# Residues of four kinds of split made by VectorE instead of GpSimd, and one softmax step issued later

## The chip, the cores and the metric

The kernel runs on one core of a Trainium2 chip. The metric is the device time of one execution in microseconds (us). Most executions of one kernel agree within 0.3%; three runs of the kernel before are given below, and one further execution was profiled.

## The reference

One inference step of a decoder layer. 1024 prompt tokens and 8 sample tokens pass through the same weights; the model is 1024 wide and everything is float32.

```python
h = rmsnorm(x, norm_mix_g);  proj = h @ w_in           # -> u, q, k, v, gate, f_low
mixed = concat(pool_mixer(u) , gla(q, k, v, log_f) * silu(gate))
x = x + mixed @ w_out
hm = rmsnorm(x, norm_mem_g); qm = hm @ w_qm            # 4 heads of 256
s = qm . mem_k * 256 ** -0.5; p = softmax(s)           # 256 memory tokens
x = x + (p @ mem_v) @ w_om
hf = rmsnorm(x, norm_ffn_g)
x = x + relu(hf @ w_up) ** 2 @ w_down                  # hidden 4096
```

For the prompt the memory's keys and values come from `mem_prompt`: `mk = mn @ w_km`, `mv = mn @ w_vm`, with `mn` the normed memory. For each of the 8 sample tokens they come from caches, `cache_mem_k` and `cache_mem_v`, of 256 tokens, 4 heads, 256 wide. The gated linear attention (`gla`) is a recurrence over chunks of 64 tokens. Outputs are the two results after a last norm, the memory's keys and values, and the recurrent states.

## The kernel before

**Arithmetic.** Every float32 operand of a large product is held as two parts in the rounded matmul format `F32R`: `hi`, the rounded value, and `lo`, the residue `x - hi`. A product is three matmuls: hi by hi, hi by lo, lo by hi. The two parts are made by `split`: ScalarE (ACT) writes `hi` (line 157), and another engine subtracts (line 158). That engine is VectorE (DVE) unless the caller passes `eng=G`, which is GpSimd (POOL).

**Stages.** After the memory's keys come two stretches that matter here. In the first, some 245 to 438 us into the span, the recurrence runs beside the last projections, the pooling mixer, the memory's values and the product with `w_out`. In the second, 438 to 627 us, cross-attention runs beside the product with `w_qm` and the start of that with `w_om`. The MLP takes the rest.

**What sets the order.** The two stretches are written as strings of steps, `GLA` and `ATTN` (lines 48 to 57). A token with a letter issues a step; a dot issues nine matmuls (six by `hi` weights, three by `lo`, 344 columns each) of the product that was begun last. Each step issues its whole chain, on all engines; a scheduler then fixes one order of instructions for each engine from what the strings recorded, and every engine works through its own list in that order. An instruction whose operand is late stops all behind it on its engine.

**Steps of the strings that are touched.** In `GLA`, `m` is `mv_unit`: 128 KB of `w_vm` for each of its two k-blocks, split 128x512 at once, and 12 matmuls into the PSUM tile `accv` (line 730); there are 16 units. In `ATTN`:

- `kH` is `load_kv`: the keys and values of head H, `kvr`, split into `kv` by two 128x1024 halves taken as one instruction.
- `VHb` is `sample_v4`: cached values of four sample tokens, DMA into `vt`, then four splits 128x512 into `vs`. There are eight, so 32 residues.
- `sHb` is `sample_scores`: VectorE multiplies cached keys `kt` with the broadcast query `qb` and sums, four instructions for each pair of sample tokens (line 856), into `ssc`.
- `wH` is `sample_p`: TensorE turns `ssc` into `ptss` (two transposes, line 862), then a softmax. `zH` is `sample_pt`: transposes of the result into `ptt` (line 895), split into `pz`. `pHn` is `sample_pv`: the sample context `psv` from `vs` and `pz` (line 911).
- `gC` begins a column block of the product with `w_qm`; its end makes `qm`, `q` and a small copy `qsm` (lines 928, 158, 933). `qC` turns `qsm` into `ptq` (line 939) and sends it to DRAM, from where `qb` is read.
- `SHt`, `THt`, `CHt` are the prompt's scores, the transposes `ptpp` with their split `pT`, and the context `accpv` (line 977). `N` is the norm's sum `pts` (line 255), read by VectorE into `v` (line 258).

Other names in the rows: `acc` with `wqmh`, `wqml` are the matmuls of the product with `w_qm` (line 194); `vt` with line 584 is the scaled value projection of the recurrence, `ws` with line 437 a sum over tiles of `w_down`, `kinv` and line 655 the opening of a chunk's scores in PSUM tile `accg`. PSUM tiles of the kinds `acc...` in `accp`, and the small ones in `mp`, have two buffers each, so a product can't begin before an older tile has been read.

Of the kernel before, what the change touches and what calls it, by code (L numbers as in the profile page):

```python
# [50 lines left out]
       "o2 a4 t2 b4 t3 . n4 m ... a5 o3 m b5 .... n5 a6 o4 b6 t4 t5 m . n6 . a7 x . m . b7 o5 ... n7 . o6 .... t6 "  # L51
       "o7 . t7 ...")
ATTN = ("g0 ..... V00 N ... k0 g1 ........ q0 g2 .. q1 .. S00 .... T00 g3 . S01 ..... C00 T01 s00 V04 . s02 . s06 "
# [7 lines left out]
def body(ctx, tc, a, o):  # L61
    nc = tc.nc
    V, A, G, PE, SY = nc.vector, nc.scalar, nc.gpsimd, nc.tensor, nc.sync
# [12 lines left out]
    def slot(shape, dt=F32, name="slot"):  # L76
        return S.tile(shape, dt, tag="s", name=name)
# [4 lines left out]
    def f(x):  # L82
        return x.bitcast(F32)
# [70 lines left out]
    def split(dst_hi, dst_lo, src, scale=None, eng=None):  # L154

        if scale is None:
            A.copy(out=dst_hi, in_=src)  # L157
            (eng or V).tensor_tensor(out=dst_lo, in0=src, in1=f(dst_hi), op=ALU.subtract)  # L158
        else:
            A.activation(out=dst_hi, in_=src, func=AF.Copy, scale=scale)  # L160
            V.scalar_tensor_tensor(out=dst_lo, in0=src, scalar=scale, in1=f(dst_hi), op0=ALU.mult, op1=ALU.subtract)
# [554 lines left out]
    def mv_unit(n):  # L716

        c, k0 = n // 4, 2 * (n % 4)
        if k0 == 0:
            mv_out["acc"] = mp.tile([P, MC, 256], F32, tag="m", name="accv")  # L720
        acc = mv_out["acc"]
        raw = wp.tile([P, 2, 256], F32, tag="raw", name="wvm", bufs=3)
        SY.dma_start(raw, a["w_vm"][0][k0 * P:(k0 + 2) * P, c * 256:(c + 1) * 256].rearrange("(k p) c -> p k c", p=P))
        hi = wp.tile([P, 2, 256], F32R, tag="whi", name="wvmh", bufs=3)
        lo = wp.tile([P, 2, 256], F32R, tag="wlo", name="wvml", bufs=3)
        split(hi, lo, raw, eng=G)
        for kk in range(2):
            for q, (x, y) in enumerate(((0, hi), (0, lo), (1, hi))):
                for m in range(MC):
                    PE.matmul(acc[:, m, :], mn[x][:, k0 + kk, m * P:(m + 1) * P], y[:, kk, :],  # L730
                              start=(k0 == 0 and kk == 0 and q == 0 and m == 0),
                              stop=(k0 == KC - 2 and kk == 1 and q == 2 and m == MC - 1), skip_group_check=True)
        if k0 == KC - 2:
            t = sm.tile([P, MC, 256], F32, tag="k2", name="mvq")
            for m in range(MC):
                A.activation(out=t[:, m, :], in_=acc[:, m, :], func=AF.Copy, scale=mr[:, 1, m:m + 1])
            SY.dma_start(mv_d[:, :, c * 256:(c + 1) * 256], t)
            SY.dma_start(o["mv"][0, 0, :, c, :].rearrange("(m p) d -> p m d", p=P), t)
# [54 lines left out]
    def out_done(acc, c, i):  # L793
# [11 lines left out]
        if c == 0:  # L805
# [3 lines left out]

    units = list(range(16))  # L810
    STEPS = {'a': gla1, 'b': gla2, 'n': gla3, 't': gla4, 'm': lambda: mv_unit(units.pop(0)), 'P': pool_out,
             'o': out_half, 'v': lambda: values_turn(3, t), 's': sample_state, 'x': sample_out}
    wpool = load_w(a["w_pool"][0].rearrange("g p c -> (g p) c"), "wpool")
# [53 lines left out]
    KV = {}  # L867

    def load_kv(h):
        kvr = tmp.tile([P, 2, 2, MT], F32, tag="t", name="kvr")  # L870
        SY.dma_start(kvr[:, 0], mkT_d[:, 2 * h:2 * h + 2, :])
        SY.dma_start(kvr[:, 1], mv_d[:, :, h * MD:(h + 1) * MD])
        KV[h] = slot([P, 2, 2, 2, MT], F32R, "kv")
        split(KV[h][:, 0], KV[h][:, 1], kvr, eng=G)

    SV, SP = {}, {}

    def sample_v4(h, *b4s):
        for b4 in b4s:
            vt = slot([P, 4, MC, MD], F32, "vt")  # L880
            for m in range(MC):
                SY.dma_start(vt[:, :, m, :],
                             a["cache_mem_v"][0, b4:b4 + 4, m * P:(m + 1) * P, h, :].rearrange("b p d -> p b d"))
            for bb in (0, 2):
                vs = SV[h, b4 + bb] = slot([P, 2, 2, MC, MD], F32R, "vs")
                for b in range(2):
                    split(vs[:, 0, b], vs[:, 1, b], vt[:, bb + b], eng=G)

    def sample_pt(h):

# [95 lines left out]
    def sample_ctx(h):  # L986
        for j in range(2):
            hi, lo = C[2 * h + j]
            split(hi[:, TP:], lo[:, TP:], VS[h][:, j, :])

    STEPS = {'g': queries_mem, 'N': lambda: tokens_sum(ss1.ss, "r2"), 'q': sample_q, 'k': load_kv, 'S': scores,
             'T': turn, 'C': context, 's': sample_scores, 'V': sample_v4, 'w': sample_p, 'z': sample_pt, 'p': sample_pv,
             'x': sample_ctx, 'O': lambda c: add_ctx(c)}

# [445 lines left out]
```

## Time and profile before

| | |
|---|---|
| three runs | 1399.91, 1406.67, 1414.76 us (median 1406.67) |
| profiled execution | 1404.68 us; its span 1403.0 us, so 1.7 us lie around the span |
| mean granted clock of TensorE | 0.982 |
| TensorE busy | 1331.8 us, 95% of the span |
| VectorE busy | 913.4 us, 65% |
| ScalarE busy | 580.6 us, 41% |
| GpSimd busy | 218.4 us, 16% |

The profile is one execution. It gives for each engine the instructions with start and duration, the idle time ahead of an instruction and what ended it, and the clock granted to TensorE; 1.00 is 2.4 GHz and 0.50 is 1.2 GHz. Engines overlap, so a busy share alone tells no cost; a wait of an engine that the end depends on does. In the stretches above that engine is TensorE: the matmuls of one product follow another with no pause except where a row shows idle time.

### The profile page before, as it was taken

How to read it: one execution, taken by the hardware profiler on the slowest of the kernel's cores; microseconds unless marked ns; L12 is line 12 of the kernel's file. 1: busy time of each engine (PE TensorE's matmuls, PEld its weight loads, DVE VectorE, ACT ScalarE, POOL GpSimd, SP SyncE). 2: the span in 40 equal slices, each digit the busy share in tenths (PEclk: the TensorE clock that was granted, in tenths of full speed). 3: DMA queues.
4: the chain of work that ended last, by engine and by line, in shares of the span. 5: the costliest groups of instructions: out<-in, count | busy, mean ns of one | idle time of the engine just before them, and what ended most of it. 6: DMA issues, size and time to landing. Idle time of an engine off the chain costs nothing. (4 is left out here: it accounts for less than half of the span.)

```text
span 1403.0 us, 22658 instructions
## 1 busy us (share of the span) xinstructions
PE 1331.8 (95%) x8734; PEld 1237.0 (88%) x8734; DVE 913.4 (65%) x1443; ACT 580.6 (41%) x1065; POOL 218.4 (16%) x229
## 2 busy tenths in 40 slices
PE   6999999899999989999999999998998999999996
PEld 6999999789999978878977799898986899999886
DVE  5776655886555577853768577677776654675663
ACT  6531122444345333533557445444445432342522
POOL 2143100331023022442200011112110000000000
PEclk9999999999999999999999999999998999999998
DMA  8846542674465436555435556555649955986671
GB/s 267 258 121 190 151 151 83 195 223 164 148 203 160 142 117 208 170 198 175 130 118 164 169 180 206 174 189 175 210 167 368 312 187 160 288 252 188 219 211 61
DMA packets 287557, 261.39 MB, mean 186 GB/s; under 512 B 13496, under 2 KB 239682, under 8 KB 287321
## 3 DMA queue, kind: packets, MB, share of 16 engines
q1 hardware_dynamic: 275289, 226.08, 52.0%
q0 software_dynamic: 6400, 21.17, 4.1%
q10 hardware_dynamic: 5760, 12.68, 2.5%
q8 instruction: 69, 1.13, 0.3%
q14 instruction: 39, 0.32, 0.1%
HBM read 195.04 MB, written 64.85 MB: 185 GB/s over the span
## 5 line engine op out<-in xcount | busy, mean ns | idle before, releaser
L1107 PE MATMUL acc<-T,wuph 128*128 128x260 f32 (+1 forms) x1408 | 288.6, 317 | 13.0 <-DVE c L1155 9.2
L1275 PE MATMUL accd<-F,wdnh 128*128 128x260 f32 (+1 forms) x1344 | 266.3, 310 | 6.1 <-ACT wdnh L157 6.1
L1107 PEld LDWEIGHTS acc<-T,wuph 128*128 128x128 f32 x1408 | 214.4, 191 | 33.8 <-ACT c L1158 5.2
L1275 PEld LDWEIGHTS accd<-F,wdnh 128*128 128x128 f32 x1344 | 201.1, 189 | 20.2 <-ACT wdnh L157 6.3
L1107 PE MATMUL acc<-T,wupl 128*128 128x260 f32 (+1 forms) x704 | 180.6, 317 | 3.6 <-DVE wupl L158 3.6
L1275 PE MATMUL accd<-F,wdnl 128*128 128x260 f32 (+1 forms) x672 | 167.4, 311 | 2.8 <-DVE wdnl L158 2.7
L1107 PEld LDWEIGHTS acc<-T,wupl 128*128 128x128 f32 x704 | 116.8, 191 | 13.1 <-DVE wupl L158 4.8
L1275 PEld LDWEIGHTS accd<-F,wdnl 128*128 128x128 f32 x672 | 109.5, 189 | 11.7 <-DVE wdnl L158 4.7
L157 ACT CAST wdnh<-wdn 128x1024 fp32r<-128x1024 f32 x52 | 54.8, 1053 | 129.8 <-PE accd L1275 124.2
L157 ACT CAST F<-fac 128x1040 fp32r<-128x1040 f32 (+2 forms) x61 | 59.9, 986 | 63.0 <-DMA fac<-fd 49.9
L158 DVE TENSOR_TENSOR F<-fac,F 128x1040 fp32r<-128x1040 f32 (+2 forms) x61 | 68.9, 1143 | 18.6 <-ACT F L157 18.0
L194 PE MATMUL acc<-c,womh 128*128 128x260 f32 (+2 forms) x384 | 80.8, 321 | 0.0
L158 DVE TENSOR_TENSOR wdnl<-wdn,wdnh 128x1024 fp32r<-128x1024 f32 x52 | 63.5, 1221 | 23.6 <-ACT wdnh L157 23.6
L194 PE MATMUL acc<-hm,wqmh 128*128 128x344 f32 x384 | 74.6, 328 | 0.0
L157 ACT CAST wuph<-w 128x512 fp32r<-128x512 f32 x64 | 38.6, 617 | 67.5 <-PE acc L1107 65.2
L194 PEld LDWEIGHTS acc<-c,womh 128*128 128x128 f32 x384 | 59.4, 188 | 6.4 <-ACT womh L157 0.8
L194 PEld LDWEIGHTS acc<-hm,wqmh 128*128 128x128 f32 x384 | 63.3, 192 | 0.6
L1111 ACT ACTIVATE c<-c 128x512 f32<-128x512 f32 (+1 forms) x64 | 40.2, 636 | 55.2 <-DVE c L1161 24.9
L158 POOL TENSOR_TENSOR vs<-vt,vs 128x512 fp32r<-128x512 f32 x32 | 47.3, 1506 | 95.2 <-ACT vs L157 91.7
L1259 DVE TENSOR_TENSOR wdn<-wdn 128x1024 f32<-128x1024 f32 x24 | 29.4, 1225 | 41.8 <-DMA wdn<-in_w_down 41.8
L194 PE MATMUL acc<-c,woml 128*128 128x260 f32 (+2 forms) x192 | 49.7, 320 | 0.0
L158 DVE TENSOR_TENSOR wupl<-w,wuph 128x512 fp32r<-128x512 f32 x64 | 42.7, 686 | 4.5 <-ACT wuph L157 4.4
(402 smaller groups left out, 2620.4 us busy)
## 6 DMA issues: line engine op xcount, KB each, us to landing
wdn<-in_w_down SPq DMA_DIRECT2D x64, 512.0 KB
fac<-fd SPq DMA_DIRECT2D x32, 520.0 KB
w<-in_w_up SPq DMA_DIRECT2D x64, 256.0 KB
ws<-in_w_down SPq DMA_DIRECT2D x48, 256.0 KB
fac<-fd SPq DMA_DIRECT2D x19, 512.0 KB
fd<-w POOLq DMA_DIRECT2D x32, 260.0 KB, 2.6
x<-xd SPq DMA_DIRECT2D x16, 516.0 KB
xd<-x SPq DMA_DIRECT2D x16, 516.0 KB
```

What stands on the lines that cost most here:

```text
L157: A.copy(out=dst_hi, in_=src)
L158: (eng or V).tensor_tensor(out=dst_lo, in0=src, in1=f(dst_hi), op=ALU.subtract)
L194: PE.matmul(acc[:, g, :c1 - c0], w, X[k][j][:, c0:c1], start=(k == 0 and i == 0), stop=(k == len(W) - 1 and i == 2))
L1107: PE.matmul(acc, w, t[k // 2][:, k % 2, j, c0:c1], start=(first and k == 0 and i == 0), stop=(k == HK - 1 and i == 2), skip_group_check=True)
L1111: A.activation(out=t, in_=t, func=AF.Relu)
L1259: V.tensor_tensor(out=raw[0], in0=raw[0], in1=raw[1], op=op)
L1275: PE.matmul(acc, W[x][:, k, :], ff[:, y, k % 2, c0:c1], start=(q == 0 and k == 0 and i == 0), stop=(q == 1 and k == UK - 1 and i == 2))
```

## The change

Two edits. `eng=G` is left out of the three calls of `split` in `mv_unit`, `load_kv` and `sample_v4`, so that 16 residues of 128x512, 4 of 128x1024 and 32 of 128x512 are VectorE's. GpSimd keeps its other work. And in `ATTN` the two tokens `w0 z0` move from behind `s04` to behind `g4 .. k1 q2 C01 ..`.

```diff
@@ ATTN @@
 ATTN = ("g0 ..... V00 N ... k0 g1 ........ q0 g2 .. q1 .. S00 .... T00 g3 . S01 ..... C00 T01 s00 V04 . s02 . s06 "
-        "s04 w0 z0 g4 .. k1 q2 C01 .. S10 .... q3 g5 p00 k2 S11 p01 q4 . s12 T10 .. s16 .. C10 s14 . T11 . x0 V10 "
+        "s04 g4 .. k1 q2 C01 .. w0 z0 S10 .... q3 g5 p00 k2 S11 p01 q4 . s12 T10 .. s16 .. C10 s14 . T11 . x0 V10 "
         "s10 . g6 C11 q5 . s20 . w1 s24 .. z1 S20 p10 k3 V14 s26 .... T20 g7 .. S21 .... s22 . T21 . C20 q7 V20 q6 "
@@ def mv_unit(n): @@
-        split(hi, lo, raw, eng=G)
+        split(hi, lo, raw)
@@ def load_kv(h): @@
-        split(KV[h][:, 0], KV[h][:, 1], kvr, eng=G)
+        split(KV[h][:, 0], KV[h][:, 1], kvr)
@@ def sample_v4(h, *b4s): @@
-                    split(vs[:, 0, b], vs[:, 1, b], vt[:, bb + b], eng=G)
+                    split(vs[:, 0, b], vs[:, 1, b], vt[:, bb + b])
```

The scheduler's lists differ in the two stretches alone. Three places matter to what follows.

TensorE, first stretch, where the first unit of the memory's values is multiplied. Before, the first two `accv` matmuls by `hi` weights are followed by this (the 27 `accv` matmuls go on to `kinv`; some rows that only repeat are left out):

```order
L730 MATMUL accv<-wvmh,mn_128 128x256 x2
L730 MATMUL accv<-wvml,mn_128 128x256 x2
L730 MATMUL accv<-wvmh,mn_129 128x256 x2
...
L730 MATMUL accv<-wvmh,mn_129 128x256
L655 MATMUL accg<-ident,kinv 128x128 x2
L521 MATMUL ptp<-ident,ul 23x128
```

and after the change by this:

```order
L730 MATMUL accv<-wvmh,mn_128 128x256 x2
L655 MATMUL accg<-ident,kinv 128x128 x2
L521 MATMUL ptp<-ident,ul 23x128
L659 MATMUL accg<-zb,kinv 128x256 x2
L529 MATMUL accp<-pr,wpoolh 128x344 x3
L529 MATMUL accp<-pr,wpooll 128x344 x3
L730 MATMUL accv<-wvml,mn_128 128x256 x2
L730 MATMUL accv<-wvmh,mn_129 128x256 x2
```

The matmuls with `kinv`, which need the PSUM tile that VectorE's `vt` (line 584) reads last, stand 27 `accv` matmuls earlier, and those are spread over the places behind them.

TensorE, second stretch, around the first head's two transposes `ptss`. Before:

```order
L977 MATMUL accpv<-pT,kv 128x512 x12
L194 MATMUL acc<-hm_3988,wqmh 128x344 x5
L862 MATMUL ptss<-ident,ssc 8x128
L194 MATMUL acc<-hm_3988,wqmh 128x344
L194 MATMUL acc<-hm_3988,wqml 128x344 x3
L194 MATMUL acc<-hm_4041,wqmh 128x344 x6
```

and after:

```order
L939 MATMUL ptq<-ident,qsm 8x128
L977 MATMUL accpv<-pT,kv 128x512 x12
L194 MATMUL acc<-hm_3988,wqmh 128x344 x6
L194 MATMUL acc<-hm_3988,wqml 128x344 x3
L194 MATMUL acc<-hm_4041,wqmh 128x344 x6
L194 MATMUL acc<-hm_4041,wqml 128x344 x3
L194 MATMUL acc<-hm_4094,wqmh 128x344 x6
L194 MATMUL acc<-hm_4094,wqml 128x344 x2
L862 MATMUL ptss<-ident,ssc 8x128
```

Between `accpv` and the first `ptss` stood 5 matmuls of 344 columns, and now stand 26; the transpose `ptq` has moved ahead of `accpv`.

VectorE, start of the second stretch, around the read of the norm's sum. Before:

```order
L281 TENSOR_TENSOR ss<-ss,sq 128x1032
L158 TENSOR_TENSOR wqml<-wqm,wqmh 128x512
L258 TENSOR_SCALAR v<-pts 128x1032
L226 TENSOR_TENSOR vt<-vt,v 128x1032
L158 TENSOR_TENSOR wqml<-wqm,wqmh 128x512
```

and after:

```order
L281 TENSOR_TENSOR ss<-ss,sq 128x1032
L158 TENSOR_TENSOR wqml<-wqm,wqmh 128x512
L158 TENSOR_TENSOR vs<-vt,vs 128x512 x4
L258 TENSOR_SCALAR v<-pts 128x1032
L158 TENSOR_TENSOR wqml<-wqm,wqmh 128x512
L226 TENSOR_TENSOR vt<-vt,v 128x1032
```

The first four residues of cached values stand ahead of `v`. The other seven sets of four stand in the same way between VectorE's older work; the second set is ahead of the first head's last `kt` instructions.

## Rows read from the trace of the kernel before

**Rows 1.** Busy time in windows: length, then busy us of PE, PEld, DVE, ACT, POOL, clock.

```profile
245.00:438.00 193.00, 184.48 (x1213) 174.43 (x1213) 125.33 (x244) 88.09 (x232) 47.47 (x39) 0.98 0.61 191
438.00:627.00 189.00, 176.20 (x1130) 161.55 (x1129) 125.68 (x296) 80.97 (x185) 57.18 (x36) 0.96 0.50 159
...
280.00:315.00 35.00, 32.15 (x210) 28.96 (x211) 28.65 (x79) 16.23 (x58) 11.98 (x13) 0.95 0.72 221
283.00:286.40 3.40, 3.40 (x16) 3.40 (x15) 1.05 (x6) 1.65 (x2) 0.93 (x1) 0.50 0.62 156
498.10:504.80 6.70, 4.91 (x18) 4.75 (x19) 5.27 (x13) 1.27 (x4) 1.10 (x1) 0.50 0.00 0
600.50:607.20 6.70, 5.82 (x28) 3.92 (x29) 3.33 (x7) 4.00 (x12) 1.49 (x2) 0.50 0.47 149
```

**Rows 2.** TensorE's waits, 245 to 438 us: total us, times, longest.

```profile
PE accv L730 <- POOL wvml L158: 2.9, 3, 1.2
PE accp L529 <- DVE rn L228: 2.3, 1, 2.3
```

**Rows 3.** TensorE's waits, 438 to 627 us.

```profile
PE ptss L862 <- DVE kt L856: 6.2, 1, 6.2
PE psv L911 <- DVE pT L158: 2.9, 1, 2.9
PE ptq L939 <- DVE qsm L933: 1.1, 1, 1.1
```

**Rows 4.** Groups by line, whole span: busy us, mean ns, idle before.

```profile
L158 POOL TENSOR_TENSOR vs<-vt,vs 128x512 fp32r<-128x512 f32 x32 | 47.3, 1506 | 95.2 <-ACT vs L157 91.7 <-issue 3.6
L158 DVE TENSOR_TENSOR wupl<-w,wuph 128x512 fp32r<-128x512 f32 x64 | 42.7, 686 | 4.5 <-ACT wuph L157 4.4
...
L158 POOL TENSOR_TENSOR wvml<-wvm,wvmh 128x512 fp32r<-128x512 f32 x16 | 22.7, 1424 | 90.8 <-ACT wvmh L157 74.6 <-issue 9.3 <-DMA wvm<-in_w_vm 5.8
...
L158 DVE TENSOR_TENSOR wd<-wdn,wd 128x1024 fp32r<-128x1024 f32 x4 | 4.9, 1225 | 3.9 <-ACT wd L157 3.9
```

**Rows 5.** The same view, VectorE alone, 438 to 627 us.

```profile
L856 DVE SCALAR_TENSOR_TENSOR kt<-kt,qb 128x256 f32<-128x256 f32 x64 | 37.2, 636 | 8.7 <-DMA kt<-in_cache_mem_k 4.7 <-DMA qb<-qdr 3.9
```

**Rows 6.** Timeline, 489 to 501 us, of TensorE, VectorE, GpSimd and ScalarE.

```profile
499.89 0.38 PE L862 MATMUL ptss<-ident,ssc 128*8 128x128 f32 x1 [6.19 <-DVE kt L856]
...
489.14 0.17 DVE L933 COPY qsm<-qm 128x8 f32<-128x8 f32 x1
491.24 1.52 DVE L856 SCALAR_TENSOR_TENSOR kt<-kt,qb 128x256 f32<-128x256 f32 x1 [1.94 <-DMA kt<-in_cache_mem_k]
...
499.41 0.41 DVE L856 SCALAR_TENSOR_TENSOR kt<-kt,qb 128x256 f32<-128x256 f32 x1
...
491.18 5.54 POOL L158 TENSOR_TENSOR vs<-vt,vs 128x512 fp32r<-128x512 f32 x4 [36.43 <-ACT vs L157]
496.68 2.52 POOL L158 TENSOR_TENSOR kv<-kvr,kv 128x1024 fp32r<-128x1024 f32 x1
...
490.48 2.19 ACT L157 CAST vs<-vt 128x512 fp32r<-128x512 f32 x4 [2.94 <-DMA vt<-in_cache_mem_v]
```

**Rows 7.** Timeline in the first stretch, TensorE and VectorE.

```profile
256.70 0.39 PE L730 MATMUL accv<-wvmh,mn 128*128 128x256 f32 x2
...
258.34 3.45 DVE L437 TENSOR_TENSOR ws<-ws 128x512 f32<-128x512 f32 x2
261.71 1.22 DVE L584 TENSOR_TENSOR vt<-acc,r 128x1032 f32<-128x1032 f32 x1
```

**Rows 8.** Timeline at the start of the second stretch: VectorE, ScalarE, TensorE.

```profile
438.70 1.23 DVE L258 TENSOR_SCALAR v<-pts 128x1032 f32<-128x1032 f32 x1 [2.28 <-PE pts L255]
...
439.00 2.19 ACT L157 CAST vs<-vt 128x512 fp32r<-128x512 f32 x4 [3.30 <-DMA vt<-in_cache_mem_v]
...
442.75 1.11 PE L194 MATMUL acc<-hm,wqmh 128*128 128x344 f32 x6
443.70 0.63 PE L194 MATMUL acc<-hm,wqml 128*128 128x344 f32 x3
```

## The prediction

> **What bounds the kernel now.** I read the table of busy time in windows first. In both stretches that the change touches TensorE is the long engine: 184.48 of 193 us and 176.20 of 189 us, with VectorE at 125 us in each [rows 1]. So time is lost or won in two ways only: TensorE's idle time, 8.5 and 12.8 us, and TensorE at its lower clock. The window table shows three stretches at 0.50 (1.2 GHz), with 3.40, 4.91 and 5.82 us of matmul time in them [rows 1]; at 1.00 (2.4 GHz) the same work takes half, so they cost some 1.7, 2.5 and 2.9 us. The second and the third of them stand right behind waits of 6.19 and 2.9 us.
>
> The table of waits names who ended each idle time. In the first stretch it is GpSimd's `wvml` for 2.9 us in three places, VectorE's `rn` for 2.3 [rows 2]. In the second it is VectorE: `kt` 6.2 us once, `pT` 2.9 once, `qsm` 1.1 once [rows 3]. The timeline around the longest one shows why VectorE was late. Its first `kt` instruction starts at 491.24 and takes 1.52 us, where one at 499.41 takes 0.41. Between the two GpSimd is busy without a break: four residues of cached values from 491.18 for 5.54 us, then `kv` from 496.68 for 2.52 [rows 6]. The group of 64 has a mean of 636 ns [rows 5], so (636 - 420) ns x 64 = 13.8 us of these rows is stretch, and what runs beside the long ones is GpSimd's subtraction. The undisturbed `qsm` copy takes 0.17 us [rows 6]; the wait of 1.1 us on another one is of the same making.
>
> **The change part by part.**
>
> *GpSimd loses 52 residues:* 47.3 + 22.7 us [rows 4] and for `kv` 4 x 2.52 [rows 6], 80 us of its time. It was idle for long in either stretch, so that by itself is worth nothing; what counts is the three waits on `wvml` and the stretched rows.
>
> *VectorE gains them.* The nearest rows are VectorE's own subtractions of the same shapes: 686 ns for 128x512 and 1225 ns for 128x1024 [rows 4]. First stretch: 16 x 0.69 = 11.0 us. Second: 32 x 0.69 + 4 x 1.23 = 27.0 us. Against it stand the stretches that go: in the second at least the 13.8 us; in the first 2.1 us for the two `ws` (3.45 us, for two at 0.69) [rows 7], and I guess 3 in all. VectorE then has about 133 of 193 and 139 of 189 us. On the mean it is far from full, so the place of each residue in its list decides.
>
> The size of what is given back can be weighed against the Trainium skill, "SBUF — State Buffer", section "Who interferes with whom": a VectorE instruction with two SBUF inputs contends with a GpSimd instruction that reads SBUF, and the one issued later is blocked for the other's whole duration. Were each of the 52 residues to block VectorE for its whole length, 80 us would come back instead of the 17 that I count, and VectorE would be lighter than before. The rows show less, since GpSimd often runs beside an idle VectorE. I keep 17.
>
> *The first head's softmax (`w0 z0` with the second set of residues).* Before, TensorE stood from 493.70 to 499.89 at `ptss` [rows 6]. After, VectorE has the four residues ahead of the last seven `kt`. The casts start when the cached values land and end at 492.67 [rows 6]; the last residue ends near 493.5. Then come one `kt` (0.35 from start to start), `q` (1.23, by `v` of the same size) and seven `kt` (2.4): 497.5. TensorE now has 21 more matmuls of 344 columns ahead of `ptss`, 0.16 us each (six from 442.75 to 443.70) [rows 8]: 3.3 us, and `ptq` 0.1, so it arrives at 497.1. It waits some 0.4 to 0.8. Of 6.19 us, 5.4 go, and with them the half clock behind it: +7.9. It keeps a lower end of 0, if `kt` or the landing is as late as now plus the residues.
>
> *`qsm`:* TensorE's wait of 1.1 us [rows 3] goes with the stretch of its copy: +1.1, at least 0. Near 563 us the fifth set of four (2.75 us) comes ahead of `pT` in VectorE's list; its neighbours there shrink too. Between -2.75 and +0.7 I take -0.3.
>
> *`psv`:* the 2.9 us for `pT` [rows 3] and the half clock behind it (2.9) are 5.8 us at most. Ahead of that `pT` stand eight `kt`, which give back some 1.7 us by the mean of the stretch, and up to 4 if they are among the long ones; but in the same stretch VectorE gets two sets of residues, 5.5 us. Between 0 and 5.8 I take +3.0, as most of those residues fall where TensorE has other work.
>
> *Start of the second stretch:* the first four residues stand ahead of `v`. Their casts end at 441.19; the last residue ends near 441.9, `v` at 443.1, where before it ended at 439.93. The product's next tile can start only then, and TensorE wanted it at 442.75 [rows 8]: -0.6, if the cached values land when they did. A later landing goes on one for one.
>
> *First stretch.* The block of 27 `accv` matmuls (0.12 us each by their 256 columns, 3.2 us) no longer covers the wait for `vt`. `vt` ended at 262.93, and some 2.2 us earlier without the stretch of `ws` [rows 7], so 260.7. TensorE arrives at 256.95, behind two matmuls from 256.70 on [rows 7], and waits 3.7 us; it is 2.3 us ahead at `kinv` but owes 3.2 us of work, -0.9. A wait of 2.9 was followed by a half clock above; I count one here, -1.7. On the other side 1.8 us of the `wvml` waits that lie further on go, the owed work can fill most of the wait on `rn` (+1.5), and the half clock at 283 us can go (+1.7). VectorE, 28.65 of 35 us busy from 280 to 315 [rows 1], gets some four residues there, 2.7 us less what GpSimd gave: -1.9. Sum +0.5, between -4.5 and +5.
>
> **Sum:** 7.9 + 1.1 - 0.3 + 3.0 - 0.6 + 0.5 = 11.6 us. The profiled execution took 1404.68 us (span 1403.0), which would become 1393.1; it lies 2.0 us below the median of the three runs, 1406.67, so against that I forecast **1395**. About 1%, 14 us either way, is what measurement can tell from no change.
>
> **Rivals.**
>
> *VectorE becomes the bound where it is densest.* Only `ptss` and `qsm` pay (7.9 + 1.1); `psv` gives nothing, the fifth set costs 1.0, the first stretch 2.8 (block and clock), the start 0.6: gain 4.6, time 1402. For it: 82% busy from 280 to 315 us, and eight sets of 2.75 us standing whole in an in-order list. Against: some 50 us of idle time on VectorE in the second stretch. The Trainium skill, "Perfetto Trace Analysis", section "Optimizing Scalar/DVE Operations", speaks this way: with a saturated VectorE, offloading even to GpSimd may make sense, though the two share an SBUF read port. By it the change would be wrong in the 82% and harmless elsewhere. Chance 0.22.
>
> *All comes back.* The 12.8 us of idle time and 5.4 us of half clock in the second stretch, less 0.6 at its start, and in the first 2.9 + 2.3 + 1.7 less 0.9: 23.6 us, so 1383; between that and 1390 if a part does. For it: most of TensorE's idle time there hangs on VectorE rows near GpSimd's. Against: waits rarely vanish whole, and every new wait of some 3 us can bring a half clock. Chance 0.18.
>
> *VectorE stands still for the cached values* (the other side). A residue waits for its cast, and the cast for `vt` from DRAM; ScalarE waited 3.30 and 2.94 us for it in two places [rows 6, 8]. GpSimd could wait with nothing behind it; VectorE has `v`, `kt`, `q` and `pT` behind. If values land later than now, so that VectorE stops some 3 us at three such places with its older work done, TensorE stops too: 9 us and a half clock behind each, 7 us; the wait at `ptss` stays, and only 3.7 us elsewhere is gained: slower by 8 to 12, with the loss in the first stretch up to 16: 1414 to 1422. It decides from a landing about 1.5 us later than now on. Against: at two places VectorE idled about 2 us then anyway, for `pts` and `kt` [rows 6, 8]. Chance 0.08.
>
> *The moved softmax does not shorten its wait,* because the residues delay `kt` by as much as `ptss` was moved: the sum less 7.9, 1403. Chance 0.07.
>
> **How the numbers follow.** My case has 0.45 and by itself reaches from 1390 to 1400. The range 1386 to 1406 takes it in, the two cases at 1402 and 1403, and half of the larger gain: 0.45 + 0.22 + 0.06 + 0.08, about 8 in 10. Faster by over 1% means under 1392.6: 0.18 and a third of my case, 0.33. Slower by over 1% means above 1420.7: a part of the third rival and what I do not see, 0.06. Same: 0.61.
>
> **What would show it.** In the profile after: no `kt` row above 0.5 us, as GpSimd is idle there; `ptss` reached near 497 us with under 1 us of idle time, and clock 1.00 behind it; no waits on `wvml` by GpSimd; a new wait of 3 to 4 us at `kinv`, on `vt`; the first matmul after the norm late by about half a microsecond; `psv` with under 2 us. I am wrong in the mechanism if `kt` stays long with GpSimd idle, and in the size if VectorE's busy time in the second stretch leaves 132 to 146 us, or if TensorE waits more than 2 us in any place where a set of four residues stands ahead of its operand.

## The result, and the profile after

| | before | after |
|---|---|---|
| median, 20 runs each | 1407.71 us | 1395.29 us |
| profiled execution | 1404.68 us | 1395.87 us |
| its span, mean granted clock | 1403.0 us, 0.982 | 1394.2 us, 0.983 |

The ratio is 0.9915, with a 95% interval of 0.9899 to 0.9930: 12 us faster. Forecast were 1395, the range 1386 to 1406, and "same within 1%" at 0.61. Two executions that took far longer, 1620.06 us of the kernel after and 3314.36 us in run 5 below, are left out of the ratios.

The busy time in windows of the profile after, with the columns of [rows 1]; 262 to 270 us is the place of a new wait, 496 to 502 that of the old longest one:

```profile
245.00:438.00 193.00, 185.50 (x1219) 176.16 (x1218) 127.88 (x260) 88.99 (x234) 23.44 (x23) 0.97 0.59 188
438.00:627.00 189.00, 185.17 (x1189) 169.16 (x1188) 133.89 (x340) 85.30 (x192) 1.28 (x1) 1.00 0.56 176
262.00:266.00 4.00, 3.34 (x12) 2.83 (x13) 3.05 (x6) 0.37 (x1) 0.79 (x2) 0.70 0.32 104
266.00:270.00 4.00, 4.00 (x30) 3.66 (x30) 3.32 (x5) 3.07 (x4) 0.00 (x0) 0.87 0.26 81
496.00:502.00 6.00, 6.00 (x40) 5.88 (x40) 6.00 (x19) 2.69 (x5) 0.00 (x0) 1.00 0.07 16
```

In the second stretch TensorE now works 185.17 of 189 us, 9 more than in [rows 1], at a clock of 1.00 throughout. In the first it is hardly denser than before, and has a new stretch at a lower clock behind 262 us.

TensorE's waits, first in the first stretch (three of its rows), then in the second. They answer to [rows 2] and [rows 3]:

```profile
PE accg L655 <- DVE vt L584: 3.3, 1, 3.3
PE accg L659 <- ACT ktok L657: 1.0, 2, 0.6
PE accg L655 <- DVE x L799: 0.9, 1, 0.9
```

```profile
PE psv L911 <- DVE pT L158: 1.2, 1, 1.2
PE accsc L954 <- DVE qm L928: 1.0, 1, 1.0
PE ptpp L967 <- DVE vs L921: 0.6, 1, 0.6
PE acc L194 <- DVE v L258: 0.6, 1, 0.6
```

The 6.2 us at `ptss` are gone, `psv` waits 1.2 instead of 2.9, `v` brings the forecast 0.6, and `kinv` waits 3.3 on `vt` where 3.7 were forecast. Why `ptss` no longer waits is in the timeline, TensorE first:

```profile
498.33 1.11 PE L194 MATMUL acc<-hm,wqmh 128*128 128x344 f32 x6
499.29 0.47 PE L194 MATMUL acc<-hm,wqml 128*128 128x344 f32 x2
499.59 0.27 PE L862 MATMUL ptss<-ident,ssc 128*8 128x128 f32 x1
```

```profile
493.12 2.48 DVE L158 TENSOR_TENSOR vs<-vt,vs 128x512 fp32r<-128x512 f32 x4
495.52 0.41 DVE L856 SCALAR_TENSOR_TENSOR kt<-kt,qb 128x256 f32<-128x256 f32 x1
...
499.43 0.07 DVE L856 DVE_READ_ACCUMULATOR kt<-kt,qb 128x1 f32 x1
499.43 1.21 DVE L158 TENSOR_TENSOR kv<-kvr,kv 128x1024 fp32r<-128x1024 f32 x1
```

VectorE makes the four residues and eight `kt` at 0.41 us each without a pause, and its last `kt` is through by 499.5. TensorE arrives at 499.59. The margin is a tenth of a microsecond.

The groups by line, whole span, that answer to [rows 4, 5]:

```profile
L856 DVE SCALAR_TENSOR_TENSOR kt<-kt,qb 128x256 f32<-128x256 f32 x64 | 23.2, 416 | 6.7 <-DMA qb<-qdr 4.0 <-DMA kt<-in_cache_mem_k 2.7
...
L158 DVE TENSOR_TENSOR vs<-vt,vs 128x512 fp32r<-128x512 f32 x32 | 20.0, 682 | 3.8 <-ACT vs L157 3.8
...
L158 DVE TENSOR_TENSOR wvml<-wvm,wvmh 128x512 fp32r<-128x512 f32 x16 | 11.0, 685 | 1.0 <-ACT wvmh L157 0.9
L158 DVE TENSOR_TENSOR kv<-kvr,kv 128x1024 fp32r<-128x1024 f32 x4 | 4.9, 1216 | 0.1
```

The added work is 20.0 + 11.0 + 4.9 = 35.9 us, but VectorE's whole busy time rose only from 913.4 to 918.6. So 30.7 us of its old rows came back, 14.0 of them in `kt` (37.2 to 23.2), of which the longest now takes 426 ns.

### The profile page after: what moved, and what is told of

Same layout as the page of the kernel before. It is cut to its first block, busy times and chain, and to the rows that moved or that the text cites. A ratio compares the mean times of both kernels' runs of the same rounds, so it can differ in the third digit from the quotient of the medians.

```text
span 1394.2 us, 22629 instructions
## 1 busy us (share of the span) xinstructions
PE 1328.1 (95%) x8734; PEld 1234.6 (89%) x8734; DVE 918.6 (66%) x1495; ACT 578.9 (42%) x1065; POOL 135.3 (10%) x177
## 5 line engine op out<-in xcount | busy, mean ns | idle before, releaser
L1024 POOL TENSOR_TENSOR ss<-ss,sq 128x512 f32<-128x512 f32 (+1 forms) x12 | 18.9, 1573 | 241.3 <-ACT sq L1022 241.3
```

The source lines that it names most:

```text
L1024: eng.tensor_tensor(out=ss2[:, cs], in0=ss2[:, cs], in1=sq, op=ALU.add)
```

## The experiments

My theory: GpSimd's subtractions stretch the VectorE instructions that run beside them, and TensorE waits behind those; VectorE has room for the residues. Rivals: the moved tokens pay; GpSimd's being busy or its writes do the harm; the first stretch gives or takes a part.

**1. The engine alone.** The changed kernel with the old text in `ATTN` (the rest of the line, which stays, is left out):

```diff
-        "s04 g4 .. k1 q2 C01 .. w0 z0 S10 .... "
+        "s04 w0 z0 g4 .. k1 q2 C01 .. S10 .... "
```

> The three residues are VectorE's, but w0 z0 stay at their old place in ATTN. The scheduler's list for TensorE then has 27 matmuls of 344 columns between accpv and ptss (5 before, 26 in the full change). Theory (GpSimd's reads no longer stretch VectorE's rows, and the scheduler itself finds other matmuls for the wait): as the full change, 1395, ratio to before 0.990 to 0.994, wait at ptss under 1 us, kt mean about 420 ns. Rival (the moved tokens are what pays at ptss): 1402 or more, with 5 us or more left at ptss.

Measured: 1393.84 us, ratio 0.9913 (0.9888 to 0.9937). There is no wait at `ptss`; `kt` has a mean of 418 ns. The moved tokens are not needed: once the residues are VectorE's, the scheduler puts 27 matmuls ahead of `ptss` by itself.

**2. The tokens alone.** The other half of the change, on the kernel before (the line cut in the same way):

```diff
-        "s04 w0 z0 g4 .. k1 q2 C01 .. S10 .... "
+        "s04 g4 .. k1 q2 C01 .. w0 z0 S10 .... "
```

> Only w0 z0 are moved; all residues stay on GpSimd. TensorE's list has 18 matmuls between accpv and ptss, 13 more than before, some 2.1 us. Theory (contention makes the wait): kt mean stays near 636 ns, the wait at ptss falls from 6.2 to about 4 us and still drops the clock, waits on pT and wvml stay: gain 1 to 3 us, 1404 to 1407, ratio 0.998 to 1.0. Rival (the move pays): the wait under 1 us and 1399 or less, ratio 0.994 or less.

Measured: 1406.89, ratio 1.0005 (0.9985 to 1.0025). TensorE's waits in the second stretch, the first three:

```profile
PE ptss L862 <- DVE kt L856: 7.2, 3, 4.2
PE psv L911 <- DVE pT L158: 4.4, 1, 4.4
PE accsc L954 <- DVE c L158: 1.9, 1, 1.9
```

The longest wait at `ptss` shrinks to 4.2 us as expected, but the second transpose then waits as well (1.5 us), and so does one of the fourth head (1.5), 7.2 us in all, and `psv` has 4.4 instead of 2.9. The stretched rows (`kt` mean 653 ns) are paid for elsewhere.

**3. Zeros instead of the cached values' residues.** On the kernel before:

```diff
-                    split(vs[:, 0, b], vs[:, 1, b], vt[:, bb + b], eng=G)
+                    A.copy(out=vs[:, 0, b], in_=vt[:, bb + b]), G.memset(f(vs[:, 1, b]), 0.0)
```

> The kernel before, but the residues of the 32 cached values are left out: GpSimd writes zeros in their place, so it writes the same bytes at the same place and reads nothing. The lists of TensorE and VectorE are those of before. kv and wvml stay on GpSimd. If GpSimd's reading stretches VectorE: kt mean 420 to 450 ns, the wait at ptss gone or under 1.5 us, psv under 1.5 us, 1395 to 1400, ratio 0.990 to 0.996. If GpSimd's being busy or its writing does it: kt mean 550 ns or more, waits as before, ratio 0.998 to 1.002.

Measured: 1392.46, ratio 0.9908 (0.9884 to 0.9933); `kt` mean 453 ns, no wait at `ptss`. That is as fast as the change, in which VectorE makes the 32 residues: their 20 us on VectorE cost nothing that can be measured (`kv` and the value weights stay on GpSimd here). My expectation erred twice: the time lies below its 1395 to 1400, and the zeros depend on no cast, so GpSimd wrote most of them early and not beside `kt`. The run shows that the residues on GpSimd were the cost, not yet whether its reads or its writes were.

**4. Writes at that place.** As before, and three more writes over each cached value, which must wait for its cast:

```diff
-                    split(vs[:, 0, b], vs[:, 1, b], vt[:, bb + b], eng=G)
+                    A.copy(out=vs[:, 0, b], in_=vt[:, bb + b]), G.memset(f(vs[:, 1, b]), 0.0), [G.memset(vt[:, bb + b], 0.0) for _ in range(3)]
```

> As the kernel with zeros in place of the cached values' residues, where most of GpSimd's writes turned out to run early, away from the kt rows. Here GpSimd also writes zeros three times over each cached value once its cast has read it, so it writes for about 1.6 us in the place and at the time of each residue, and reads nothing. The residues are again left out; the lists of TensorE and VectorE are those of before. If reading is what stretches the two-input rows: kt mean under 470 ns with rows of 0.41 to 0.43 us right beside the writes, no wait over 1 us at ptss, 1391 to 1398, ratio 0.989 to 0.995. If writing does it as well: kt rows over 0.8 us beside the writes, a wait at ptss of 3 us or more, ratio 0.997 or more. Single-input rows (qsm, pp) may be stretched by writes: those that had 0.42 and 0.69 us, for 0.17 and 0.37, in the kernel with zeros lay beside a write.

Measured: 1390.70, ratio 0.9879 (0.9853 to 0.9904). The timeline of GpSimd and, in the second fence, of VectorE at the first head's `kt`:

```profile
492.76 5.69 POOL L887 MEMSET vt<- 128x512 f32 x12 [14.84 <-ACT vs L887]
498.40 2.39 POOL L158 TENSOR_TENSOR kv<-kvr,kv 128x1024 fp32r<-128x1024 f32 x1
```

```profile
492.81 0.43 DVE L856 SCALAR_TENSOR_TENSOR kt<-kt,qb 128x256 f32<-128x256 f32 x1 [0.96 <-DMA kt<-in_cache_mem_k]
...
493.50 0.42 DVE L856 SCALAR_TENSOR_TENSOR kt<-kt,qb 128x256 f32<-128x256 f32 x1
...
496.37 0.42 DVE L856 SCALAR_TENSOR_TENSOR kt<-kt,qb 128x256 f32<-128x256 f32 x1
```

GpSimd is busy for 5.69 us, as long as with the four subtractions of [rows 6], and not one `kt` is stretched. The same run holds the counterpart, a `kt` beside the `kv` subtraction, which stays on GpSimd (VectorE's timeline, then GpSimd's):

```profile
551.97 2.57 DVE L856 SCALAR_TENSOR_TENSOR kt<-kt,qb 128x256 f32<-128x256 f32 x1
...
551.72 2.54 POOL L158 TENSOR_TENSOR kv<-kvr,kv 128x1024 fp32r<-128x1024 f32 x1 [5.27 <-ACT kv L157]
```

It is the reading. The Trainium skill, "SBUF — State Buffer", section "Who interferes with whom", says the same: a VectorE instruction with two SBUF inputs contends with a GpSimd instruction that reads SBUF, not with one that only writes. This run agrees, at 0.42 us beside writes against 1.52 beside subtractions.

**5. The contention put back.** On the changed kernel GpSimd makes the residues a second time, for nobody:

```diff
-            vt = slot([P, 4, MC, MD], F32, "vt")
+            vt, tw = slot([P, 4, MC, MD], F32, "vt"), sm.tile([P, MD], F32, tag="tw", name="tw", bufs=1)
...
-                    split(vs[:, 0, b], vs[:, 1, b], vt[:, bb + b])
+                    split(vs[:, 0, b], vs[:, 1, b], vt[:, bb + b]), [G.tensor_tensor(out=tw, in0=vt[:, bb + b, m], in1=f(vs[:, 0, b, m]), op=ALU.subtract) for m in range(MC)]
```

> The changed kernel, and GpSimd also makes the 32 residues of the cached values a second time into a scratch tile that nobody reads (64 subtractions of 128x256). The lists of TensorE and VectorE are those of the changed kernel; nothing waits for the extra work but the buffers it reads. Theory (the stretch comes from GpSimd's subtractions beside VectorE's rows): kt or the residues next to it stretched again, kt mean 500 ns or more, VectorE busy in the second stretch up by 10 to 25 us, a wait of 2 us or more at ptss or psv, time 1402 to 1415, ratio to before 0.997 to 1.005. Rival (what pays is that VectorE has less far to wait for, or the order; contention is small): 1395 to 1398, ratio 0.991 to 0.994.

Measured: 1413.56, ratio 1.0050 (1.0027 to 1.0072). GpSimd's timeline, then VectorE's, then TensorE's:

```profile
494.58 8.74 POOL L887 TENSOR_TENSOR tw<-vt,vs 128x256 f32<-128x256 f32 x8 [44.55 <-ACT vs L157]
```

```profile
494.89 4.43 DVE L158 TENSOR_TENSOR vs<-vt,vs 128x512 fp32r<-128x512 f32 x4
499.24 0.95 DVE L856 SCALAR_TENSOR_TENSOR kt<-kt,qb 128x256 f32<-128x256 f32 x1
...
500.12 1.75 DVE L158 TENSOR_TENSOR q<-qm,q 128x1032 fp32r<-128x1032 f32 x1
```

```profile
505.05 0.38 PE L862 MATMUL ptss<-ident,ssc 128*8 128x128 f32 x1 [3.53 <-DVE kt L856]
```

TensorE and VectorE have the very lists of the changed kernel. The residues take 4.43 us instead of 2.48, `q` 1.75 instead of 1.22, and TensorE waits 3.53 us at `ptss` where it waited none; the whole gain is lost and more. Not all of the loss need be contention: GpSimd's second set also holds the buffers that it reads, and what that costs was not measured.

**6. and 7. The first stretch apart.** The memory's value weights go back to GpSimd in the changed kernel (6), or are the only ones on VectorE in the kernel before (7):

```diff
-        split(hi, lo, raw)
+        split(hi, lo, raw, eng=G)
```

> The changed kernel with the 16 residues of the memory's value weights back on GpSimd. In the first stretch all lists are those of before, with the block of 27 accv matmuls ahead of kinv; in the second they are those of the change. Theory (the first stretch gives nothing, all is won in the second): as the full change within 2 us, 1393 to 1398, ratio to before 0.990 to 0.994. Rival (first stretch loses, by the new wait of 3.3 us at kinv): 1390 or less. Rival (it gains, by the wvml waits that went): 1399 or more.

> The kernel before, and only the 16 residues of the memory's value weights are VectorE's. The lists of the first stretch are those of the changed kernel, those of the second are those of before. Theory (first stretch worth nothing): ratio 0.9985 to 1.0015, 1404 to 1408; the wait at kinv is 3 to 4 us, those on wvml are gone; kt mean stays near 636 ns and 6 us stay at ptss. Rivals: 1402 or less (first stretch gains), 1410 or more (it loses).

Measured: 1392.54, ratio 0.9904 (0.9868 to 0.9939), and 1405.22, ratio 0.9995 (0.9973 to 1.0018). The second stretch alone makes the whole gain; of the first no gain or loss is shown, with an interval in run 7 from 3.8 us gained to 2.5 lost. In the second of these kernels the waits on `wvml` are gone and the 3.3 us at `kinv` are there.

**8. to 11. Further.** Three kernels move more of GpSimd's reading to VectorE: the sums of squares (8), the other half of the memory's key weights (9), both (10), and both with the value weights back on GpSimd (11). The lines edited:

```diff
-                eng = V if self.n == KC - 1 else G
+                eng = V
...
-            eng = V if c == KC - 1 else G
+            eng = V
...
-            split(w[:, 0, ks], w[:, 1, ks], raw, eng=(V, G)[i])
+            split(w[:, 0, ks], w[:, 1, ks], raw, eng=V)
```

> The changed kernel, and the sums of squares (line 281 in the first stretch, 6 of 128x1032; line 1024 beside the product with w_om, 12) are VectorE's too, so that GpSimd subtracts or adds nothing beside attention. TensorE's list is unchanged. Theory (taking GpSimd's reads away pays only where TensorE waits for a stretched row): TensorE has under 1 us of waits where line 1024 runs and none named by line 281, so 0 to 2 us: 1393 to 1396, ratio 0.990 to 0.993. Rival (every microsecond of GpSimd's reading costs): 1388 or less.

> The changed kernel, and the 8 residues of the memory's key weights that GpSimd makes (the other 8 are VectorE's already; their mean is 819 ns where the shape takes 0.69) are VectorE's too. There TensorE waits 0.6 us for GpSimd's wk, 2.0 for mkT and 1.8 for mg, both VectorE's. Theory (stretched rows in front of a wait pay): 0 to 3 us better than the change, 1391 to 1395. Rival (VectorE is dense there, 161 of 245 us, and the added 5.5 us stand in line): slower than the change by 1 to 4.

> The changed kernel with both further steps, the key weights' other 8 residues and the sums of squares on VectorE. If the two gains add (some 5 and 2 us against the change): 1386 to 1390, ratio to before 0.985 to 0.989. If they are the same microseconds, or noise of the runs: 1390 to 1394.

> As the one before, with the residues of the memory's value weights on GpSimd, which gives the first stretch its old lists and its block of accv matmuls ahead of kinv. Theory (first stretch worth nothing): within 2 us of it. If the wait at kinv costs more than the waits on wvml: 2 to 4 us faster.

> The changed kernel itself, so that the two others are compared with it on the same chip: 1393 to 1397, ratio 0.990 to 0.993.

| | median us | ratio to before, interval |
|---|---|---|
| 8, sums | 1391.82 | 0.9896 (0.9861 to 0.9930) |
| 9, key weights | 1389.83 | 0.9889 (0.9849 to 0.9928) |
| 10, both | 1392.26 | 0.9904 (0.9881 to 0.9928) |
| 11, both, value weights back | 1390.05 | 0.9884 (0.9856 to 0.9912) |
| the change again, beside 10 and 11 | 1392.70 | 0.9905 (0.9883 to 0.9928) |

All intervals overlap with that of the change. None of the steps is shown to gain. 8 and 9 came out below what I expected (1393 to 1396, and 1391 to 1395), and their apparent gains do not add in 10. Whether 11 is a microsecond or two faster than the change stays open: its four executions (1388.55 to 1390.37) all lie below the four of 10 (1391.89 to 1393.69), which hints that the value weights are a little better left on GpSimd.

## Why the prediction was right

Each term can be read from the start of one and the same matmul in the two traces, after less before. Between two marks TensorE has the same matmuls in both kernels. The terms are what this difference gains or loses between two marks:

| mark | before | after | difference | term, measured | forecast |
|---|---|---|---|---|---|
| first `accv` matmul | 256.70 | 258.56 | +1.86 | | |
| `pts`, line 255 | 436.76 | 438.52 | +1.76 | first stretch +0.1 | +0.5 |
| third block of `w_qm` | 454.11 | 456.73 | +2.62 | start -0.9 | -0.6 |
| sixth block of `w_qm` | 519.96 | 514.22 | -5.74 | `ptss` and clock +8.4 | +7.9 |
| seventh block of `w_qm` | 541.77 | 534.30 | -7.47 | `qsm` +1.7 | +1.1 |
| first matmul of `w_om` | 586.88 | 579.75 | -7.13 | fifth set of residues -0.3 | -0.3 |
| first matmul of the MLP | 706.93 | 695.00 | -11.93 | `psv` and clock +4.8 | +3.0 |
| last matmul | 1391.29 | 1381.80 | -9.49 | | |

The terms sum to 13.8 us, where 11.6 were forecast. The two ends are not the change's work. Ahead of the first mark both kernels have the same instructions, but for GpSimd's first `wvml` at 250.88, and the 1.8 us by which this run lay behind were there at 106 us already. The instructions of the MLP are the same. The profiles of runs 1, 6, 8 and 9 enter the MLP 11.3 to 12.8 us ahead of the kernel before and end it 8.4 to 15.2 us ahead, with the same instructions in it. So the last microseconds of one profile say nothing on the change; the 20 runs give 12.4 us. That the time was hit to 0.3 us is luck: the terms together were 2.2 us too small, the base was a median of three, and single executions of the kernel after lie from 1392.91 to 1400.64.

*`ptss`.* The path was forecast well, 497.1 for TensorE's arrival; less the 2.62 us by which this run lay behind, it arrived at 497.0. Two things differ. No wait is left, where 0.4 to 0.8 was forecast: less the 2.62 us, the casts of the second set began 1.1 us earlier than before. And I called it the moved softmax: run 1 shows that the move adds nothing to the engine's change, and run 2 that alone it is worth nothing. The rows of the two orders on which I built the term were right, but I put their cause in the wrong edit: the list of run 1, with the tokens in their old place, has 27 matmuls there. What made the wait was the stretch: run 3 keeps the old list, with five matmuls ahead of `ptss`, and has no wait. The added matmuls cover the residues that VectorE now makes itself.

*`qsm` and the start.* The 0.6 us over the forecast at `qsm` are a wait of `accpv` on `c` that is gone too. At the start of the stretch 443.1 less 442.75 is 0.35, not the 0.6 that I wrote; `v` ended 0.4 us later than counted, so that the hit of 0.6 is luck.

*`psv`.* The term was mis-sized by 1.8 us. I kept half of 5.8, since two sets of residues come into that stretch. 1.2 us of the wait are left, but no lower clock follows, so that the clock came back whole: 1.7 + 2.9. The mark also holds what I had not counted, a wait of `accsc` on `c` that is gone (1.1) and a new one at `ptpp` (0.6).

*What comes back.* I counted 17 us, the rows give 30.7: VectorE is busy for 127.88 and 133.89 us in the two stretches, where 133 and 139 were forecast. By the exclusive lock of the Trainium skill, "SBUF — State Buffer", section "Who interferes with whom", it would have been 80 if each residue had blocked VectorE for its whole length. Row by row the kernel before agrees: behind the first `kt` of 1.52 us, VectorE gets one `kt` through for each of GpSimd's other three subtractions, and the fifth beside `kv` of 2.52 us.

```profile
492.70 1.50 DVE L856 SCALAR_TENSOR_TENSOR kt<-kt,qb 128x256 f32<-128x256 f32 x1
...
496.93 2.55 DVE L856 SCALAR_TENSOR_TENSOR kt<-kt,qb 128x256 f32<-128x256 f32 x1
```

But VectorE was idle for some 22 of GpSimd's 80 us (added up from the starts and ends of both engines' rows before), and part of the rest passed beside instructions with fewer SBUF inputs, so less came back.

*First stretch.* The new wait at `kinv` (3.3), the half clock behind it, and the waits on `wvml` and `rn` and the half clock at 283 us that vanish are all there, and they cancel: +0.1 in the table. One loss was not forecast: from 355 to 363 us the granted clock is 0.57 where it was 0.79. Run 7 has it too (0.57), run 6 has not (0.84); what brings it was not looked into.

*The rivals.* VectorE did not become the bound: in run 3 the work is not on VectorE at all, and the time is the same. The cached values did not land later by the 1.5 us that the third rival needs: against the same matmuls the first set's casts began 0.2 us later than before and the second's 1.1 earlier. ScalarE's longest wait for them was 3.5 us, and that shows as 0.6 us at `v` alone. Nor did all come back: 1.2 us at `psv` and 3.3 at `kinv` are left.

## What to carry to other kernels

GpSimd is not a free second VectorE: before giving it elementwise work, compare VectorE's rows beside it with the same rows alone, for the instruction that another engine waits for may be the stretched neighbour (here 1.52 us for 0.42). Where VectorE has idle time in the stretch, it makes the residues in half the time, and its own work then costs nothing that can be measured. When a scheduler sets the order, an edit of the engine changes the order too, so run each edit alone before naming the one that pays; of the two here one did nothing.

## What the runs showed of the hardware

That reads do the harm and writes do none was not known from the kernel before. But it holds only for instructions with two SBUF inputs. In run 4 the four `pp` multiplications by a per-row scalar, of one SBUF tensor, lay beside writes of GpSimd (VectorE's timeline, then GpSimd's):

```profile
564.13 1.97 DVE L836 TENSOR_SCALAR pp<-pp,su 128x256 f32<-128x256 f32 x4
```

```profile
563.94 1.14 POOL L887 MEMSET vs<- 128x512 f32 x2 [2.62 <-PE acc L194]
565.35 1.21 POOL L887 MEMSET vs<- 128x512 f32 x2 [0.27 <-PE acc L194]
```

They take 1.97 us. All 32 of them in the profile after, where GpSimd is idle, by minimum, median and maximum in ns:

```profile
L836 DVE TENSOR_SCALAR pp<-pp,su x32: 323/348/355, 469.1 to 597.2; 128x256 f32<-128x256 f32 x32
```

Four at 348 ns would be 1.39 us or less, while `kt` beside such writes kept its 0.42. So a write of GpSimd delays some one-input instructions and spares the two-input ones; a read delays the two-input ones.

GpSimd is delayed too. Its four `zb` copies (line 652), in the kernel before, with VectorE's two-input sums `ws` from 254.04 on beside them, and in the second fence after, with the one-input reciprocal beside them up to 255.98:

```profile
253.99 3.34 POOL L652 COPY zb<-qd 64x256 f32<-64x256 f32 x4
...
254.04 3.03 DVE L437 TENSOR_TENSOR ws<-ws 128x512 f32<-128x512 f32 x4
```

```profile
254.41 1.76 POOL L652 COPY zb<-qd 64x256 f32<-64x256 f32 x4
...
249.38 6.60 DVE L572 RECIPROCAL ge<-ge 128x1032 f32<-128x1032 f32 x1 [1.59 <-ACT ge L571]
255.90 2.62 DVE L437 TENSOR_TENSOR ws<-ws 128x512 f32<-128x512 f32 x4
```

The copies take 3.34 us there and 1.76 here, and `ws` 3.03 against 2.62 in the profile after: each side pays for the other.
